# A kernel's activations in SBUF are allocated 64 bytes further from its weights

## The chip, the cores and the metric

The kernel runs on one core of a Trainium2 chip. The metric is the device time of one execution in microseconds (us). Three executions of the kernel before took 1510.82, 1510.87 and 1511.72 us, a median of 1510.87 us.

## What is computed

One layer of a hybrid decoder on 256 tokens of width 2048, in float32, and a final RMSNorm. Cut to its steps, the reference is:

```python
mod = silu(c) @ w_ada + b_ada           # shift1, scale1, gate1, shift2, scale2, gate2
h   = rms_norm(x, g_norm1) * (1 + scale1) + shift1
p   = h @ w_in                          # retention q,k,v,g | HGRN2 q,f,i,g | gates A, B
y_a = (layer_norm(retention(rope(q), rope(k), v)) * silu(g)) @ w_ret_o
y_b = (head_rms_norm(hgrn2(silu(q), f, i)) * silu(g)) @ w_hg_o
x   = x + gate1 * ((sigmoid(ga) * y_a + sigmoid(gb) * y_b) @ w_out)
h2  = rms_norm(x, g_norm2) * (1 + scale2) + shift2
a, b = split(causal_conv3(h2 @ w_up))   # w_up is 2048 x 11264
x   = x + gate2 * ((silu(a) * b) @ w_down)
out = rms_norm(x, g_final)
```

The weights are about 95 million float32 values, each read once (382 MB).

## The kernel before

**How a product is formed.** Weights and activations are both float32. Each is split into an upper part, which is the value rounded to the type float32r, and a lower part, which is what the rounding left out. A product is then three matmuls in float32r: upper activations by upper weights, lower activations by upper weights, and upper activations by lower weights. The upper and lower part of an activation lie side by side in one tile, for two blocks of 128 rows of the contraction: `hT` (after the first norm), `og` and `mT` (in the branches and their merge), `h2T` (after the second norm) and `gs` (in front of the down projection), each 128 partitions by 4096 bytes. The upper and lower parts of a weight piece are the tiles `wh` and `wl`, each also 128 by 4096 bytes, for two blocks of 128 rows and 512 columns.

**The flow of a weight piece.** `load` (L155) starts a DMA from HBM into a tile `raw` on the queue of SyncE. `upper` (L161) lets ScalarE copy it to `wh` with rounding (L169). `rest` (L172) lets VectorE subtract that from `raw` into `wl` (L174). `pieces` (L178) strings these together, `products` (L250) passes the pieces to one of the matmul helpers. A `raw` tile is free for its next load when L174 has read it; a `wh` or `wl` tile is free when the last matmul has read it.

**The matmul helpers.** In each, a matmul has a stationary operand, which a weight load brings into the array first, and a moving operand, which streams through it.

- `mm_rows` (L192): activations are stationary (128 columns), weights move (512 columns). L198 takes the upper activations, L199 the lower, both with `wh`; L203 takes the upper activations with `wl`. Most of the input projections and all of the output, merge and down projections use it.
- `mm_cols` (L205): weights stationary, activations moving, 256 columns (L214, L215, L218).
- `mm_wide` (L220): weights stationary, upper and lower activations together moving, 512 columns (L225), then the upper ones alone with `wl`, 256 columns (L228).
- `up_group` (L1110), the up projection: for each block of 128 rows and two column slices of the weights, two matmuls with `wh` and 512 moving columns (L1125) and two with `wl` and 256 (L1127).

So every one of these matmuls has one operand in a weight tile and one in an activation tile, and the weight load of the next matmul runs beside the stream of the current one.

**Other work.** The six modulation vectors are formed on VectorE by dot products (L458) that read a row of the modulation weights in `raw` and the vector `sc`. Retention and HGRN2 run in between on all engines, with float32 matmuls of their own that read activations alone: L711 multiplies a 128 by 128 block of scores (`at`) with the values (`p`), L713 another such block (`a`, from a pool of smaller tiles) with the same kind of values.

**Where the tiles lie.** SBUF is handed out pool after pool, and in a pool slot after slot, in the order in which a slot's tag is first used, each start rounded up to 32 bytes. All offsets are bytes within each partition. The constants come first, up to byte 17,440. Then comes the pool of weights, `self.wp` (L62): 12 slots of `raw`, each 4,128 bytes because the longest row has 1,025 float32 values, up to byte 66,976; then 4 slots of `wh` and 4 of `wl`, 4,096 bytes each, up to byte 99,744. There the pool of activations starts, `self.sb` (L63): 27 slots of 4,096 bytes (`blk`, L75) that hold all the activation tiles named above, then the smaller tiles (`small`, `s1`, `s2`).

The first `wh` slot and the first activation slot are therefore 32,768 bytes apart, 8 times 4,096. The slices that matmuls take start at multiples of 512 bytes within their tiles. So the starts of the two operands of any weight matmul are a multiple of 512 bytes apart.

The instructions are ordered by the program text, with the interleaved work metered by `pump` (L129); no step looks at an address.

Of the kernel before, what the change touches and what calls it, by code (L numbers as in the profile page):

```python
# [12 lines left out]
F32 = mybir.dt.float32  # L13
# [6 lines left out]
P = 128  # L20
# [37 lines left out]
class Kernel:  # L58
# [735 lines left out]
    def run(self):  # L794
# [29 lines left out]
        def take(g, ps, fresh):  # L824
            for at, z in self.parts(ps, ATT[g] in ROWS):
                dst = accs[g][:, at, :]
                if fresh:
                    nc.scalar.activation(dst, z, AF.Copy)
                else:
                    nc.vector.tensor_tensor(dst, dst, z, ALU.add)  # L830
# [44 lines left out]
        def begin(kind, hb, *ins):  # L875
            att.append(self.start(kind(hb, *ins, gates)))

        small = False
        while min(done) < KT:
            if work > SMALL and not small:  # L880
                small = True
                self.small_loads(nc.sync, ("freq", "lbT", "lmask"))
                self.start(self.trig())
                self.start(self.lower_bound())
            have = min(KT, 2 + int((work - LAG) / ADA_EVERY))
            m = have - done[g]
            if m > 0:
                self.finish(*ada[:have])
                if g < RESIDENT:
                    self.products(mms[g], ps[g], a["wa"][g], act, done[g], m, first=False, last=have == KT)  # L890
                    if have == KT:
                        take(g, ps[g], True)
                else:
                    take(g, self.products(mms[g], self.pg(), a["wa"][g], act, done[g], m), done[g] == 0)
                done[g] = have
                work += m
                if have == KT and ATT[g] in GATES:
                    nc.scalar.activation(accs[g], accs[g], AF.Silu)
                    gates[GATES.index(ATT[g])] = accs[g]
                for hb in range(2):  # L900
                    gs = [hb, 2 + hb, 4 + hb]
                    if g in gs and min(done[i] for i in gs) == KT:
                        self.pace(0, 14.0, 24)
                        begin(self.hgrn, hb, *(accs[i] for i in gs))
                        for i in gs:
                            accs[i] = None
            else:
                work += 0.5
            g = (g + 1) % len(ATT)
            if have == KT and done[0] < KT:  # L910
                g = min(i for i in range(len(ATT)) if done[i] < KT)
        self.xT = None
        v = accs[10:]
        del accs
# [377 lines left out]
```

## Time and profile before

| | |
|---|---|
| median of three executions | 1510.87 us |
| the profiled execution | 1511.24 us |
| its span, first to last instruction | 1509.5 us |
| PE (TensorE matmul) busy | 1493.7 us, 8,466 matmuls |
| PEld (weight load) busy | 1275.5 us |
| DVE (VectorE) busy | 1211.9 us |
| ACT (ScalarE) busy | 841.7 us |
| read from HBM | 382.11 MB, 255 GB/s over the span |
| mean granted TensorE clock | 0.998 |

The profiled execution is the one whose trace the sections below quote. Its span is 1.7 us shorter than its own time. A busy time counts the stretches in which at least one instruction of the engine is under way. A matmul's duration runs from its start to the modelled end of its output, so successive matmuls overlap in the trace: a mean of 395 ns does not mean that one starts each 395 ns. The rate is read from the chain of waits, which gives each matmul the time from its predecessor's end to its own.

### The profile page before, as it was taken

What the parts mean: (1) busy time and instruction counts of PE and PEld (TensorE: products, weight loads), DVE (VectorE), ACT (ScalarE), POOL (GpSimd) and SP (SyncE); (2) the same over time, 40 slices, a digit from 0 to 9 for tenths busy, and PEclk for the clock granted to TensorE, in tenths of its full rate; (3) what the DMA queues carried; (4) which work ended last, traced back from release to release, by engine and by line L of the source; (5) the groups of instructions that cost most, each with busy time, mean ns of one, the idle gap of its engine ahead of it and who ended that gap; (6) DMA issues with size and microseconds to landing.
All of it is one profiled execution on the core that took longest, in us unless ns stands there. A gap on an engine that the chain in (4) does not pass through costs nothing.

```text
span 1509.5 us, 22703 instructions
## 1 busy us (share of the span) xinstructions
PE 1493.7 (99%) x8466; PEld 1275.5 (84%) x8466; DVE 1211.9 (80%) x1647; ACT 841.7 (56%) x1210; POOL 4.0 (0%) x8
## 2 busy tenths in 40 slices
PE   8999999999999999999999999999999999999997
PEld 6889899888888888888888888888888888888886
DVE  7899997998999877898977778777777769455784
ACT  6745456767775644455466555555555658344342
POOL 0000000000000000000000000000000000000000
PEclk9999999999999999999999999999999999999999
DMA  9999997777887899989847777777777666667651
GB/s 373 376 347 336 321 320 257 265 248 274 281 278 262 285 302 326 318 290 361 298 132 242 229 233 230 230 231 238 229 239 231 216 193 204 197 206 212 183 171 56
DMA packets 110994, 385.71 MB, mean 256 GB/s; under 512 B 12802, under 2 KB 13346, under 8 KB 110884
## 3 DMA queue, kind: packets, MB, share of 16 engines
q1 hardware_dynamic: 110016, 383.14, 76.7%
q8 instruction: 66, 1.08, 0.3%
q10 hardware_dynamic: 868, 1.13, 0.2%
q14 instruction: 44, 0.36, 0.1%
HBM read 382.11 MB, written 2.11 MB: 255 GB/s over the span
## 4 chain that ended last, share of the span: by engine, by line
PE 93%; DVE 3%; ACT 1%; issue 1%; DMA 1%; SPq 0%; DVEq 0%; ACTq 0%
PE pg L198 13%; PE pg L203 13%; PE pg L199 13%; PE po L1125 11%; PE pg L1125 10%; PE po L1127 5%; PE pg L1127 5%; PE pg L225 4%; PE po L198 3%; PE po L203 3%; PE po L199 3%; PE pg L228 2%; DVE wl L174 1%; DVE raw L458 1%; PE po L218 1%
## 5 line engine op out<-in xcount | busy, mean ns | idle before, releaser
L174 DVE TENSOR_TENSOR wl<-raw,wh 128x1024 fp32r<-128x1024 f32 (+1 forms) x536 | 633.1, 1191 | 233.6 <-ACT wh L169 230.6
L169 ACT ACTIVATE wh<-raw 128x1024 fp32r<-128x1024 f32 (+1 forms) x536 | 547.9, 1033 | 482.5 <-PE pg L199 167.0
L458 DVE SCALAR_TENSOR_TENSOR raw<-raw,sc 128x1024 f32<-128x1024 f32 x192 | 233.8, 1222 | 0.1
L1125 PE MATMUL po<-h2T,wh 128*128 128x512 f32 x704 | 221.1, 395 | 0.0
L1125 PE MATMUL pg<-h2T,wh 128*128 128x512 f32 x688 | 216.4, 396 | 0.0
L198 PE MATMUL pg<-wh,hT 128*128 128x512 f32 x512 | 202.1, 395 | 0.9 <-DVE p L830 0.6
L199 PE MATMUL pg<-wh,hT 128*128 128x512 f32 x512 | 199.8, 390 | 0.0
L1127 PEld LDWEIGHTS po<-h2T,wl 128*128 128x128 f32 x704 | 132.3, 188 | 31.3
L1127 PEld LDWEIGHTS pg<-h2T,wl 128*128 128x128 f32 x688 | 129.2, 188 | 31.0 <-DVE wl L174 0.5
L203 PE MATMUL pg<-wl,hT 128*128 128x512 f32 x512 | 138.4, 390 | 0.1
L1127 PE MATMUL po<-h2T,wl 128*128 128x256 f32 x704 | 138.3, 278 | 0.0
L1127 PE MATMUL pg<-h2T,wl 128*128 128x256 f32 x688 | 135.3, 278 | 0.1
L198 PEld LDWEIGHTS pg<-wh,hT 128*128 128x128 f32 x512 | 96.1, 188 | 21.3 <-ACT f L579 1.0
L203 PEld LDWEIGHTS pg<-wl,hT 128*128 128x128 f32 x512 | 96.0, 188 | 20.6 <-DVE wl L174 0.4
L199 PEld LDWEIGHTS pg<-wh,hT 128*128 128x128 f32 x512 | 96.2, 188 | 19.6 <-DVE hT L387 0.3
L1125 PEld LDWEIGHTS po<-h2T,wh 128*128 128x128 f32 x704 | 107.2, 189 | 0.0
L1125 PEld LDWEIGHTS pg<-h2T,wh 128*128 128x128 f32 x688 | 104.7, 189 | 0.0
L199 PE MATMUL pg<-wh,gs 128*128 128x512 f32 x176 | 68.6, 390 | 0.0
L198 PE MATMUL pg<-wh,gs 128*128 128x512 f32 x176 | 68.5, 389 | 0.0
L198 PE MATMUL po<-wh,gs 128*128 128x512 f32 x176 | 68.5, 389 | 0.0
L199 PE MATMUL po<-wh,gs 128*128 128x512 f32 x176 | 68.5, 389 | 0.0
L225 PE MATMUL pg<-hT,wh 128*128 128x512 f32 x256 | 65.1, 396 | 0.2 <-DVE p L247 0.2
(255 smaller groups left out, 2023.3 us busy)
## 6 DMA issues: line engine op xcount, KB each, us to landing
raw<-in_wup SPq DMA_DIRECT2D x176, 512.0 KB, 4.5
raw<-in_wdown SPq DMA_DIRECT2D x88, 512.0 KB, 4.2
raw<-in_wa SPq DMA_DIRECT2D x80, 512.0 KB, 5.7
raw<-in_ada SPq DMA_DIRECT2D x64, 512.5 KB, 5.4
raw<-in_ada SPq DMA_DIRECT2D x64, 512.0 KB, 5.5
raw<-in_wab SPq DMA_DIRECT2D x64, 512.0 KB, 5.0
raw<-in_gate SPq DMA_DIRECT2D x32, 512.5 KB, 4.3
raw<-in_wk SPq DMA_DIRECT2D x32, 512.0 KB, 5.1
```

The source lines that it names most:

```text
L169: self.pin(self.nc.scalar.activation(wh, raw, AF.Copy))
L174: self.last = self.nc.vector.tensor_tensor(wl, raw, wh.bitcast(F32), ALU.subtract)
L198: nc.tensor.matmul(ps[t], lhsT=act[:, hi], rhs=wh, start=first and i == 0, stop=False)
L199: nc.tensor.matmul(ps[t], lhsT=act[:, lo], rhs=wh, start=False, stop=False)
L203: nc.tensor.matmul(ps[t], lhsT=act[:, hi], rhs=wl, start=False, stop=last and i == len(items) - 1)
L218: nc.tensor.matmul(outs[j], lhsT=wl[:, cs[j]], rhs=act[:, :T], start=False, stop=last and i == len(items) - 1, skip_group_check=True)
L225: nc.tensor.matmul(ps[z], lhsT=wh[:, z * P : (z + 1) * P], rhs=act, start=first and i == 0, stop=False)
L228: nc.tensor.matmul(ps[z][:, :T], lhsT=wl[:, z * P : (z + 1) * P], rhs=act[:, :T], start=False, stop=last and i == len(items) - 1)
L458: dot = self.pin(nc.vector.scalar_tensor_tensor(raw[:, 0, :], raw[:, 0, :], 1.0, self.sc[:, u * GW : u * GW + w], ALU.mult, ALU.mult, accu ...
L1125: self.pin(nc.tensor.matmul(ps[j + z], lhsT=wh[:, cs[z]], rhs=act, start=kt == 0, stop=False, skip_group_check=bool(begun)))
L1127: nc.tensor.matmul(ps[j + z][:, :T], lhsT=wl[:, cs[z]], rhs=act[:, :T], start=False, stop=kt == KT - 1, skip_group_check=bool(begun))
```

## The change

After the loop of the input projections, `run` takes one more tile from the pool of weights, 128 partitions by 16 float32 values, 64 bytes. Nothing writes or reads it.

```diff
@@ -909,6 +909,7 @@
             g = (g + 1) % len(ATT)
             if have == KT and done[0] < KT:
                 g = min(i for i in range(len(ATT)) if done[i] < KT)
+        self.wp.tile([P, 16], F32, name="gap")
         self.xT = None
         v = accs[10:]
         del accs
```

Its tag is new to the pool, so it gets a slot of its own behind the last `wl` slot, at byte 99,744, and every tile of the pool of activations starts 64 bytes later: the first activation slot is at byte 99,808, which is 8 times 4,096 and 64 bytes behind the first `wh` slot. Constants, `raw`, `wh`, `wl` and PSUM stay where they were. The last tile of the pool still ends within the same memory.

On each engine the list of instructions is the same as before, row by row: 5,592 rows on TensorE, 1,421 on VectorE, 1,158 on ScalarE, 764 on the queue of SyncE and 12 on GpSimd, with the same operations, shapes, waits and tile slots. What differs is the running number in tiles' names behind that point, the line numbers below L911, which are one higher, and the start addresses of the activation tiles.

## The prediction

> **What bounds the kernel now.** I read the page's totals and shares of the chain first, then the table by stage, the groups by shape, and the chain itself for the rate of the matmuls.
>
> ```profile
> span 1509.5 us, 22703 instructions
> PE 1493.7 (99%) x8466; PEld 1275.5 (84%) x8466; DVE 1211.9 (80%) x1647; ACT 841.7 (56%) x1210; POOL 4.0 (0%) x8
> ...
> PE 93%; DVE 3%; ACT 1%; issue 1%; DMA 1%; SPq 0%; DVEq 0%; ACTq 0%
> ```
>
> TensorE is under way in 1493.7 of 1509.5 us, and 93% of the chain that ended last are its matmuls. Only 15.8 us are not covered by it.
>
> ```profile
> 20.00:300.00 280.00, 278.33 (x1584) 245.04 (x1583) 251.24 (x329) 165.66 (x232) 1.91 (x2) 1.00 0.91 322
> ...
> 768.00:1185.00 417.00, 416.90 (x2418) 364.50 (x2417) 321.97 (x499) 240.63 (x367) 0.00 (x0) 1.00 0.72 226
> 1185.00:1509.50 324.50, 316.78 (x1501) 265.30 (x1499) 213.66 (x248) 154.12 (x199) 0.00 (x0) 0.99 0.59 180
> ```
>
> These are rows of the table by stage: stretch, its length, then busy time of PE, PEld, DVE, ACT and POOL, the granted clock, the DMA share and GB/s. In the input projections (20 to 300 us), in the up projection (from 768 us) and in the down projection, TensorE has the whole stretch but for 1.7, 0.1 and 7.7 us, the last being mostly the tail after the final matmul. The clock is full. No other engine is near its limit but VectorE in the first of these (251 of 280). So the time can change by more than about 1% only if the matmuls themselves start at another rate. How fast do they start?
>
> ```profile
> 299.98 0.84 PE pg L228 x7
> 300.81 1.84 PE pg L225 x8
> ...
> 1494.53 1.81 PE po L203 x8
> ```
>
> ```profile
> 900.01 0.46 PE po L1125 x2
> 900.48 0.23 PE po L1127 x2
> 900.71 0.47 PE po L1125 x2
> 901.18 0.23 PE po L1127 x2
> ...
> 905.59 0.46 PE pg L1125 x2
> ```
>
> These are rows of the chain: start, time taken, and what. 8 matmuls of 512 columns take 1.81 us, 0.2263 each; 7 of 256 columns take 0.84, 0.120 each. Twice the latter less the former is 0.0137 us: what each matmul costs beside its columns, 13.7 ns. In the up projection two of each kind should take 2 x 0.2263 + 2 x 0.120 = 0.6926 us. From 900.01 to 905.59 there are 16 rows, 8 such fours: 0.6975 each, about 0.005 more. This surplus and the 13.7 ns are the two places where a matmul may be waiting for its own operands.
>
> **The change part by part.** The extra tile has no instruction, no load and no semaphore, and each engine's list is the same row by row. So nothing is removed, added or moved past a queue, and the sum has no term for an instruction. What is left is the address of the activations: absolute (64 bytes more) and relative to the weights and the constants. It can act only where an instruction's duration depends on addresses. I go through the kinds.
>
> *VectorE and ScalarE on weights.* Their operands lie in one pool and move in no way.
>
> ```profile
> L174 DVE TENSOR_TENSOR wl<-raw,wh x536: 670/1224/1271, 17.4 to 1491.1; 128x1024 fp32r<-128x1024 f32 x167, 128x512 fp32r<-128x512 f32 x12
> ...
> L169 ACT ACTIVATE wh<-raw x536: 616/1062/1074, 15.3 to 1490.0; 128x1024 fp32r<-128x1024 f32 x167, 128x512 fp32r<-128x512 f32 x12
> ...
> L458 DVE SCALAR_TENSOR_TENSOR raw<-raw,sc x192: 1194/1221/1261, 10.9 to 1186.3; 128x1024 f32<-128x1024 f32 x96, 128x1025 f32<-128x1025 f32 x96
> ```
>
> Here stand shortest, median and longest duration in ns. They also test the question itself. The 12 `raw` slots are 4,128 bytes apart, so from slot to slot the distance to `wh`, `wl` and `sc` shifts by 32 bytes beyond a multiple of 4,096; over the slots all distances modulo 128 occur in equal number, the 64 bytes of this change among them. If one in four were slower or faster the medians would not lie this near one end: 1,224 of at most 1,271 for L174 (its low end is the half-sized form), 1,221 between 1,194 and 1,261 for L458. So VectorE and ScalarE do not feel such a distance by more than about 3%, and where they work on activations I cost the shift at zero. The cover is TensorE's 99%: VectorE has 29 us free between 20 and 300 us, and 3% of its 251 us is 7.5.
>
> *DMA.* Nearly all bytes go to `raw`, which stays; the few loads and stores of activations keep their sizes. Zero, between -1 and +1 us for the last stores in the tail.
>
> *TensorE on weights.* All of the weights' matmuls, some 7,470 of the 8,466, pair a weight tile with an activation tile. Today their starts are a multiple of 512 bytes apart, then a multiple of 512 and 64. No row of this trace shows that distance with float32r operands, so I bound it. The nearest row by address is in the branch:
>
> ```profile
> 358.50 0.39 PE L711 MATMUL po<-p,at 128*128 128x128 f32 x2
> 358.73 0.39 PE L713 MATMUL po<-p,a 128*128 128x128 f32 x2
> 358.95 0.39 PE L711 MATMUL po<-p,at 128*128 128x128 f32 x2
> 359.17 0.39 PE L713 MATMUL po<-p,a 128*128 128x128 f32 x2
> ```
>
> In L711 both operands are in 4,096-byte slots, a multiple of 512 bytes apart. In L713 the stationary one is in a smaller pool whose slots lie 32 bytes off that grid modulo 64 and 96 modulo 128. Both lines take 0.39 us for two and start 0.22 to 0.23 us apart. So the distance does not matter there. The nearest row by kind is the down projection: within a tile L198, L199 and L203 use stationary slices at 0, 512, 1024 and 1536 bytes, and the 1.81 us for 8 has no room for a slow one among them. I take zero, the value of both nearest rows. The weakness is that the first is float32 and slower per column, and the second moves by 512 only, so an effect that repeats within 512 bytes would be hidden.
>
> By the Trainium skill, "TensorE: Matmul & The Clock Gate", section "Step-by-step: what each phase is for", TensorE has two independent read ports into SBUF, one for the moving operand and one for the weight load, so a weight load takes nothing from the running matmul; by that rule the distance is free and the sum is zero. The same page's "Back-to-back issue gap" gives 2.5 ns beside the columns at the full clock; this trace shows 13.7, so here the trace does not agree.
>
> *Sum.* 0 on 1511.24 us, the profiled execution's own time (its span and 1.74 us around it). That execution lies 0.37 us above the median of the three, within their spread of 0.9, so the forecast for the median is **1510.9 us**.
>
> **The rivals.**
>
> *Somewhat faster: the surplus goes.* The 0.005 us in each four of the up projection, and its like elsewhere, could be weight loads that meet the stream at the same low addresses, as all now do.
>
> ```profile
> L1125 PE MATMUL po<-h2T,wh 128*128 128x512 f32 x704 | 221.1, 395 | 0.0
> L1125 PE MATMUL pg<-h2T,wh 128*128 128x512 f32 x688 | 216.4, 396 | 0.0
> L198 PE MATMUL pg<-wh,hT 128*128 128x512 f32 x512 | 202.1, 395 | 0.9 <-DVE p L830 0.6 <-ACT p L828 0.2
> L198 PE MATMUL po<-wh,gs 128*128 128x512 f32 x176 | 68.5, 389 | 0.0
> L225 PE MATMUL pg<-hT,wh 128*128 128x512 f32 x256 | 65.1, 396 | 0.2 <-DVE p L247 0.2
> ```
>
> These are groups by shape: total and mean ns of one. There are (704 + 688) / 2 = 696 fours: 696 x 0.005 = 3.5 us. L225 takes 1.84 us for 8 against 1.81: 32 x 0.03 = 1 us. L198 on `hT` has a mean of 395 against 389 on `gs`: 512 x 0.006 = 3 us. Together 7.5. That gives 1507.4 for the up projection alone and 1503.4 for all. For it: such a surplus appears in lines where the activations move. Against it: L198 on `hT` has it too and is of the other kind, and in the up projection 512 and 256 columns alternate, so it may be the alternation.
>
> *Much faster: the 13.7 ns go.* If each weight load now delays the stream because both read the same place, the shift could end that: at most 7,470 x 0.0137 = 102 us, 1409 us. For it: the distance is the same for every weight matmul, as is the cost. Against it: L711 and L713. By the page's figure of 2.5 ns instead of none, it would be about 84 us, an estimate.
>
> *Slower: the weight load meets the stream where it didn't.* The place is every steady run of L198 to L203 and L214 to L228, which now has the clean rate. It decides from the point where one more matmul in each four is delayed as in the up projection: 0.005 / 4 = 0.00125 us on the 7,470 - 2,784 = 4,690 other matmuls, 5.9 us, 1516.8. If instead each took the 0.23 of L225's rows (1.84 / 8), 0.0037 x 5,000 matmuls of 512 columns, 18.5 us, 1529.4. For it: with all starts on one grid a weight load keeps a fixed place relative to the stream, and the clean rate may rest on that place. Against it: the same rows as above.
>
> *The change does not do what it says.* The tile could be placed where it shifts nothing. The start addresses in the built program speak against it; the time would be 1510.9.
>
> **How the numbers follow.** The addresses do not matter: 0.51, with 0.03 for the shift that isn't one, together 0.54 at 1510.9. Somewhat faster 0.20, at 1503.4 to 1507.4. Much faster 0.06. Slower 0.20, of which I put two thirds at 1516.8 and a little beyond. A measurement of this kernel can tell about 0.2%, 3 us, from no change; both ends of the first rival and of the third are past that, so faster is 0.26, same 0.54, slower 0.20. The range goes from the first rival's far end, less a little, to the third's near end and 2 us for its spread: 1503 to 1519. Outside lie the much faster case and the far third of the slower one, 0.06 + 0.07 = 0.13.
>
> **What would show it.** In the changed kernel's chain, 8 matmuls of L203 should take 1.81 us again and the fours of the up projection 0.6975. The first rival is right if the fours fall towards 0.693 and L198's mean on `hT` towards 389; the second if L203's 8 fall below 1.81, towards 1.72; the third if they rise, or if L199's mean passes 389. L174, L169 and L458 should keep 1,224, 1,062 and 1,221. The forecast is wrong if, with an identical list of instructions, TensorE's busy time in the up or down projection changes by more than 1 us. It would also be wrong, for another reason, if the 7.7 us that the last stretch leaves uncovered grew, since no operation there changed.

## The result and the profile after

The changed kernel took 1524.64 us (median of four executions, 1524.3 to 1525.71) against 1511.21 us for the kernel before on the same chips: a ratio of 1.009, 95% interval 1.0077 to 1.0102. It is slower, by 13.4 us. The forecast was no change, 1510.9 us, with a range of 1503 to 1519 that does not hold the time.

The page of the changed kernel, its totals and shares of the chain:

```profile
span 1522.8 us, 22703 instructions
PE 1507.6 (99%) x8466; PEld 1273.4 (84%) x8466; DVE 1212.3 (80%) x1647; ACT 841.6 (55%) x1210; POOL 4.0 (0%) x8
...
PE 96%; ACT 2%; DVE 1%; issue 0%; DMA 0%; SPq 0%; DVEq 0%; ACTq 0%
```

VectorE and ScalarE are busy as long as before, to 0.4 us, and the granted clock is 0.998 in both kernels. TensorE is busy 13.9 us longer with the same 8,466 matmuls, and the span is 13.3 us longer. So no wait was added: matmuls themselves start later after one another. Rows of the chain (start, time taken, what) show which:

```profile
300.54 1.83 PE pg L225 x8
302.37 0.91 PE pg L228 x8
...
1507.66 1.87 PE po L203 x8
```

```profile
900.16 0.46 PE po L1126 x2
900.62 0.23 PE po L1128 x2
...
905.68 0.46 PE po L1126 x2
```

Eight matmuls of L203 take 1.87 us instead of 1.81, those of L225 1.83 instead of 1.84. The up projection (lines L1126 and L1128 here) has 16 rows from 900.16 to 905.68, eight fours in 5.52 us: 0.690 each instead of 0.6975. One kind of line became slower, the other faster. The groups by shape, total us and mean ns of one, agree:

```profile
L1126 PE MATMUL po<-h2T,wh 128*128 128x512 f32 x704 | 218.4, 392 | 0.0
L198 PE MATMUL pg<-wh,hT 128*128 128x512 f32 x512 | 204.5, 399 | 0.9 <-ACT wh L169 0.6 <-ACT p L828 0.3
L198 PE MATMUL po<-wh,gs 128*128 128x512 f32 x176 | 70.0, 398 | 0.0
L199 PE MATMUL po<-wh,gs 128*128 128x512 f32 x176 | 69.2, 393 | 0.0
L225 PE MATMUL pg<-hT,wh 128*128 128x512 f32 x256 | 65.1, 397 | 0.3 <-DVE p L247 0.3
```

L198 on `gs` went from 389 to 398 ns, L1126 from 395 to 392. The operations that split the weights, on operands that did not move against each other, kept their medians (shortest, median and longest ns):

```profile
L174 DVE TENSOR_TENSOR wl<-raw,wh x536: 665/1224/1260, 17.1 to 1504.1; 128x1024 fp32r<-128x1024 f32 x167, 128x512 fp32r<-128x512 f32 x12
L169 ACT ACTIVATE wh<-raw x536: 613/1062/1074, 14.7 to 1503.0; 128x1024 fp32r<-128x1024 f32 x167, 128x512 fp32r<-128x512 f32 x12
```

For a balance I took, for each matmul of both traces, the time from its start to the start of the next, subtracted before from after, and added up by helper; such a time includes whatever the next matmul waited for. The up projection is that of `up_group`. The same balance is used for the experiments below (all in us, against the trace of before):

| kernel | mm_rows (3,360) | mm_cols (768) | mm_wide (512) | up projection (2,784) | others | sum |
|---|---|---|---|---|---|---|
| changed kernel | +20.4 | -1.7 | -0.5 | -4.5 | -0.4 | +13.3 |
| e1_all_shift | 0.0 | -0.1 | 0.0 | 0.0 | -0.1 | -0.2 |
| e2_room | +0.1 | 0.0 | 0.0 | 0.0 | -0.2 | -0.1 |
| e3_nearer64 | +6.3 | -4.1 | -0.4 | -2.3 | 0.0 | -0.5 |
| e4_sweep32 | +16.8 | -1.5 | +0.4 | +2.4 | 0.0 | +18.0 |
| e5_rows_back | +0.2 | -1.3 | -0.6 | -4.6 | 0.0 | -6.5 |
| e6_up_only | +0.1 | -0.1 | 0.0 | -4.6 | -0.2 | -4.7 |
| e7_best | +0.2 | -1.9 | -0.6 | -4.6 | -0.2 | -7.2 |
| e8_sweep_fine | +17.5 | -1.2 | +0.1 | +2.0 | -0.1 | +18.2 |
| e9_gap128 | +18.8 | -0.8 | +0.4 | 0.0 | -0.4 | +18.1 |
| e10_dist256 | 0.0 | +1.1 | 0.0 | 0.0 | +0.1 | +1.1 |
| e11_up_wl | +0.1 | -0.1 | 0.0 | -2.3 | 0.0 | -2.3 |
| e12_up_wh | +0.1 | 0.0 | 0.0 | +1.1 | -0.3 | +0.8 |

In the changed kernel the lines with stationary activations lost 20.4 us, 6.1 ns a matmul, and those with stationary weights won 6.7 back.

### The profile page after: what moved, and what is told of

Read it like the earlier page. It is cut to its first block, busy times and chain, and to the rows that moved or that the text cites. A ratio compares the mean times of both kernels' runs of the same rounds, so it can differ in the third digit from the quotient of the medians.

```text
span 1522.8 us, 22703 instructions
## 1 busy us (share of the span) xinstructions
PE 1507.6 (99%) x8466; PEld 1273.4 (84%) x8466; DVE 1212.3 (80%) x1647; ACT 841.6 (55%) x1210; POOL 4.0 (0%) x8
## 4 chain that ended last, share of the span: by engine, by line
PE 96%; ACT 2%; DVE 1%; issue 0%; DMA 0%; SPq 0%; DVEq 0%; ACTq 0%
PE pg L198 14%; PE pg L199 14%; PE pg L203 14%; PE po L1126 11%; PE pg L1126 10%; PE po L1128 5%; PE pg L1128 5%; PE pg L225 4%; PE po L198 3%; PE po L203 3%; PE po L199 3%; PE pg L228 2%; PE po L214 1%; PE po L215 1%; PE po L218 1%; PE pg L214 1%
## 5 line engine op out<-in xcount | busy, mean ns | idle before, releaser
L174 DVE TENSOR_TENSOR wl<-raw,wh 128x1024 fp32r<-128x1024 f32 (+1 forms) x536 | 632.7, 1189 | 242.1 <-ACT wh L169 239.8
L169 ACT ACTIVATE wh<-raw 128x1024 fp32r<-128x1024 f32 (+1 forms) x536 | 547.8, 1033 | 498.2 <-PE pg L199 186.9
L1126 PE MATMUL po<-h2T,wh 128*128 128x512 f32 x704 | 218.4, 392 | 0.0
L1126 PE MATMUL pg<-h2T,wh 128*128 128x512 f32 x688 | 213.9, 392 | 0.0
L198 PE MATMUL pg<-wh,hT 128*128 128x512 f32 x512 | 204.5, 399 | 0.9 <-ACT wh L169 0.6
L199 PE MATMUL pg<-wh,hT 128*128 128x512 f32 x512 | 202.7, 396 | 0.0
L1128 PEld LDWEIGHTS po<-h2T,wl 128*128 128x128 f32 x704 | 132.2, 188 | 29.1
L1128 PEld LDWEIGHTS pg<-h2T,wl 128*128 128x128 f32 x688 | 129.1, 188 | 29.0 <-DVE wl L174 0.6
L203 PE MATMUL pg<-wl,hT 128*128 128x512 f32 x512 | 141.5, 395 | 0.0
L1128 PE MATMUL po<-h2T,wl 128*128 128x256 f32 x704 | 138.9, 279 | 0.0
L1128 PE MATMUL pg<-h2T,wl 128*128 128x256 f32 x688 | 136.0, 279 | 0.1
L198 PEld LDWEIGHTS pg<-wh,hT 128*128 128x128 f32 x512 | 96.1, 188 | 24.0 <-ACT wh L169 1.0
L203 PEld LDWEIGHTS pg<-wl,hT 128*128 128x128 f32 x512 | 96.0, 188 | 23.4
L199 PEld LDWEIGHTS pg<-wh,hT 128*128 128x128 f32 x512 | 96.1, 188 | 22.7 <-DVE hT L387 0.2
L1126 PEld LDWEIGHTS po<-h2T,wh 128*128 128x128 f32 x704 | 106.6, 188 | 0.0
L1126 PEld LDWEIGHTS pg<-h2T,wh 128*128 128x128 f32 x688 | 104.2, 188 | 0.0
L198 PE MATMUL po<-wh,gs 128*128 128x512 f32 x176 | 70.0, 398 | 0.0
L198 PE MATMUL pg<-wh,gs 128*128 128x512 f32 x176 | 70.0, 398 | 0.0
L199 PE MATMUL pg<-wh,gs 128*128 128x512 f32 x176 | 69.3, 393 | 0.0
L199 PE MATMUL po<-wh,gs 128*128 128x512 f32 x176 | 69.2, 393 | 0.0
L225 PE MATMUL pg<-hT,wh 128*128 128x512 f32 x256 | 65.1, 397 | 0.3 <-DVE p L247 0.3
```

The source lines that it names most:

```text
L169: self.pin(self.nc.scalar.activation(wh, raw, AF.Copy))
L174: self.last = self.nc.vector.tensor_tensor(wl, raw, wh.bitcast(F32), ALU.subtract)
L198: nc.tensor.matmul(ps[t], lhsT=act[:, hi], rhs=wh, start=first and i == 0, stop=False)
L199: nc.tensor.matmul(ps[t], lhsT=act[:, lo], rhs=wh, start=False, stop=False)
L203: nc.tensor.matmul(ps[t], lhsT=act[:, hi], rhs=wl, start=False, stop=last and i == len(items) - 1)
L225: nc.tensor.matmul(ps[z], lhsT=wh[:, z * P : (z + 1) * P], rhs=act, start=first and i == 0, stop=False)
```

## The experiments

A time that is given without a ratio is that of a single execution; the kernel before took 1511.1 us (median) beside each of these groups of runs.

**Distance or place?** Two theories fit this. By the distance theory, the rate of a weight matmul depends on how far its two operands lie apart. By the place theory, it depends on where the activations lie, whatever the weights do. e1_all_shift moves both pools by the same 64 bytes:

```diff
+        c.tile([P, 16], F32, name="gap")
         self.silu = []
```

> The 64 bytes are put among the constants, so weights and activations both start 64 bytes later and their distance is that of before. Distance theory (a weight matmul's rate depends on the distance between its stationary and its moving operand): as before, 1511 us, L198 on gs 389 ns mean, L1125 395 to 396. Place theory (the rate depends on where the activations lie, whatever the weights do): as the changed kernel, 1524.6 us, L198 on gs 398, L1125 392.

It took 1510.96 us beside 1511.13 for the kernel before. Its groups are those of before:

```profile
L1126 PE MATMUL po<-h2T,wh 128*128 128x512 f32 x704 | 221.1, 395 | 0.0
...
L198 PE MATMUL po<-wh,gs 128*128 128x512 f32 x176 | 68.5, 389 | 0.0
```

The activations lie exactly where the changed kernel has them, and nothing is slower. The place theory falls.

**A base in which the distance can be set.** To set distances by helper, the slots of `wh` and `wl` get room, and each piece starts at an offset in its slot:

```diff
-        raw = self.wp.tile([P, m, w], F32, name=f"raw_{self.n}", tag="raw", bufs=12)
+        raw = self.wp.tile([P, m, w], F32, name=f"raw_{self.n}", tag="raw", bufs=11)
...
+    def offset(self, kind):
+        return "", {}.get(kind, 0)
+    def place(self, name, tag, o, m, w):
+        z = self.wp.tile([P, 2 * G + 128], F32R, name=f"{name}_{self.n}", tag=tag, bufs=4)
+        return z[:, o : o + m * w].rearrange("p (m w) -> p m w", m=m)
...
+        z, o = self.offset(kind)
+        wh = self.place("wh" + z, "wh", o, m, w)
+        wl = self.place("wl" + z, "wl", o, m, w)
```

`kind` says which helper will use the piece: rows, cols, wide or up. Offsets count float32 values, so 16 is 64 bytes. A weight that starts further into its slot lies nearer to the activations behind it: an offset of 192 or 448 bytes leaves the activations 64 bytes beyond a multiple of 256, as in the changed kernel. In these kernels L198, L199 and L203 have become L207, L208 and L212, and L1125 and L1127 have become L1135 and L1137.

> Gives each wh and wl slot 512 bytes more (4608 instead of 4096) and takes one of the twelve raw slots for it; the distances stay multiples of 512, and 32 bytes among the constants keep the weights' own place modulo 512. Both theories: 1511 us within 2 us, L198 on gs 389, L1125 395 to 396. It is the base for the next two; if the eleventh raw slot costs, it shows here.

1511.18 us, with all five columns of the balance within 0.2 us of before. The missing `raw` slot costs nothing.

**The other direction.** e3_nearer64 puts all weights at 64 bytes: `{"rows": 16, "cols": 16, "wide": 16, "up": 16}`.

> As e2_room, but weights start 64 bytes further into their slots in all stages, so that the activations lie 64 bytes nearer to them instead of further. Distance theory with a sign (the changed kernel slowed the lines with stationary activations by 4 to 9 ns a matmul and sped up those with stationary weights by 2 to 4): the roles are exchanged; L1125 should be slower than before and the lines L198 to L203 faster or at least not slower, about 1500 to 1512 us. Distance theory without a sign: as the changed kernel, 1524 us, L198 on gs 398. Place theory: as before, 1511 us, since no activation moved.

1510.64 us. The simple exchange of roles did not happen, and neither did the changed kernel's loss:

```profile
L1135 PE MATMUL po<-h2T,wh 128*128 128x512 f32 x704 | 219.6, 393 | 0.0
...
L208 PE MATMUL po<-wh,gs 128*128 128x512 f32 x176 | 69.0, 392 | 0.0
...
L207 PE MATMUL po<-wh,gs 128*128 128x512 f32 x176 | 68.9, 391 | 0.0
```

`mm_rows` is slower than before, but by 6.3 us and not by 20.4; the up projection and `mm_cols` are faster. A time equal to that of before hides a loss and gains of the same size. The direction of the distance matters, but not as a mirror.

**A sweep in one execution.** e4_sweep32 lets the offset go through 16 values of 32 bytes each from piece to piece and puts a letter into the tiles' names, so that the profile keeps them apart.

```diff
+        i = self.turns = getattr(self, "turns", -1) + 1
+        i = (5 * i + i // 16) % 16
+        return "ABCDEFGHIJKLMNOP"[i], 8 * i
```

> As e2_room, but each weight piece starts at another of 16 offsets in its slot, 0 to 480 bytes in steps of 32 (letters A to P in the names wh and wl). Distance theory: the groups of one line by letter differ, for L198 on gs between at least 389 (A) and 398 (448 bytes, letter O, the distance of the changed kernel), and the letters that are best for stationary activations are not those that are best for stationary weights (L1125). Place theory: all letters of a line have the same mean, within 1 ns.

1529.0 us. Rows for the matmuls with `wl` and `hT` (L214 here; shortest, median, longest ns) and groups of the up projection (L1137 here; total us, mean ns), by letter:

```profile
L214 PE MATMUL pg<-wlI,hT x30: 389/389/397, 34.6 to 584.1; 128*128 128x512 f32 x30
L214 PE MATMUL pg<-wlC,hT x36: 388/392/398, 40.2 to 589.7; 128*128 128x512 f32 x36
L214 PE MATMUL pg<-wlK,hT x36: 388/392/397, 65.3 to 567.4; 128*128 128x512 f32 x36
L214 PE MATMUL pg<-wlB,hT x38: 393/395/397, 46.2 to 553.5; 128*128 128x512 f32 x38
L214 PE MATMUL pg<-wlJ,hT x36: 393/396/400, 117.1 to 575.8; 128*128 128x512 f32 x36
```

```profile
L1137 PE MATMUL po<-h2T,whA 128*128 128x512 f32 x48 | 15.0, 394 | 0.0
L1137 PE MATMUL po<-h2T,whC 128*128 128x512 f32 x48 | 15.2, 397 | 0.0
L1137 PE MATMUL po<-h2T,whG 128*128 128x512 f32 x40 | 12.4, 392 | 0.0
L1137 PE MATMUL po<-h2T,whK 128*128 128x512 f32 x40 | 12.6, 397 | 0.0
L1137 PE MATMUL po<-h2T,whO 128*128 128x512 f32 x48 | 14.9, 392 | 0.0
```

The letters differ. Letters eight places apart, 256 bytes, agree: C with K, B with J, G with O. In L214, with stationary activations, 0 and 256 bytes (A, I) are the best, and the odd multiples of 32 are among the slow ones. With stationary weights 192 and 448 (G, O) are better than 0. G also repeats the loss of the changed kernel, though no activation moved: L198 and L199 on `gs` (L209 and L210 here) have medians of 398 and 393 ns, the means of the changed kernel.

```profile
L209 PE MATMUL pg<-whG,gs x12: 392/398/398, 1279.8 to 1440.0; 128*128 128x512 f32 x12
L210 PE MATMUL pg<-whG,gs x12: 388/393/393, 1280.0 to 1440.2; 128*128 128x512 f32 x12
```

By the spacing of starts within a piece, a four of the up projection takes 696 ns at A, 690 at G and 706 at F; `mm_cols` seemed best at C and at G, 113 ns a matmul against 120 at A. The means of one letter are contaminated by neighbouring pieces that lie elsewhere, so only kernels with one distance a helper, as below, give clean figures.

**The loss undone, the gain kept.** If distance it is, one can have the old distance for `mm_rows` and the new one for the rest.

```diff
+        return "", {"cols": 48, "wide": 48, "up": 48}.get(kind, 0)   # e5_rows_back
+        return "", {"up": 48}.get(kind, 0)                           # e6_up_only
+        return "", {"cols": 16, "wide": 48, "up": 48}.get(kind, 0)   # e7_best
```

> As e2_room, with the weights of mm_cols, mm_wide and the up projection starting 192 bytes into their slots (for these the distance of the changed kernel, if the pattern repeats every 256 bytes as the letters of e4_sweep32 do: A like I, G like O) and those of mm_rows at 0, the distance of before. Distance theory: the changed kernel without its loss. L198 on gs back at 389, L1125 near 392 as there; 1511.2 less the 6 to 7 us that the lines with stationary weights gained, 1504 to 1506 us. Place theory: 1511, as no activation moved.

1504.67 us, a ratio to before of 0.9955 (0.9939 to 0.9971). It beats both kernels, by 6.4 us and by 20 us, with the same 8,466 matmuls.

```profile
L1135 PE MATMUL po<-h2T,wh 128*128 128x512 f32 x704 | 218.4, 392 | 0.0
...
L207 PE MATMUL po<-wh,gs 128*128 128x512 f32 x176 | 68.5, 389 | 0.0
```

> As e2_room, with only the up projection's weights at 192 bytes. Distance theory: the up projection's share alone, 4 to 5 us off, 1506 to 1507 us; all other lines as in e2_room. If the gain of one stage is given back by another that starts earlier (loads that come late), less than 2 us.

1506.7 us, 0.9971 (0.9958 to 0.9985): 4.4 us off, as large as the up projection's own column, 4.6. Nothing is given back.

> As e5_rows_back, but the weights of mm_cols at 64 bytes, where letter C of e4_sweep32 gave starts 113 ns apart instead of 120. Distance theory: 768 matmuls x 4 to 7 ns more, 3 to 5 us below e5_rows_back, 1500 to 1502 us. If the input projections, where VectorE is busy 90% of the time and the DMA engines 91%, can't use a faster TensorE, no difference to e5_rows_back.

1504.73 us, 0.9958 (0.9944 to 0.9972), no better than e5_rows_back. The reason is not the one offered: `mm_cols` itself hardly became faster. In the rows of its first line (L223; shortest, median, longest ns), e5_rows_back, e7_best and then e3_nearer64, which has the same 64 bytes there:

```profile
L223 PE MATMUL pg<-hT,wh x128: 279/279/415, 21.2 to 264.4; 128*128 128x256 f32 x128
```

```profile
L223 PE MATMUL pg<-hT,wh x128: 276/281/281, 20.7 to 263.6; 128*128 128x256 f32 x128
```

```profile
L223 PE MATMUL pg<-hT,wh x128: 276/276/342, 21.1 to 263.0; 128*128 128x256 f32 x128
```

At one and the same distance, the median is 281 in e7_best and 276 in e3_nearer64. The two also differ in where the pieces of `mm_rows` lie, whose matmuls alternate with those of `mm_cols` in stretches of about 100 to 200. That does not explain it: by the spacing of starts, the first stretch of `mm_cols`, before any matmul of `mm_rows`, already has a median of 118 ns in e7_best and of 114 in e3_nearer64. Of the four long stretches after it, e7_best has three at 118 and one at 114, e3_nearer64 all four at 113. And the sweep's 113 ns for G, the distance of `mm_cols` in e5_rows_back, became 118 there. So at one distance, in one execution, a run of matmuls can keep either of two rates, and the distance alone does not fix the rate. What picks one is not shown.

**Finer steps.** e8_sweep_fine is e4_sweep32 with other offsets.

```diff
-        return "ABCDEFGHIJKLMNOP"[i], 8 * i
+        return "ABCDEFGHIJKLMNOP"[i], (0, 1, 2, 3, 4, 12, 15, 16, 17, 20, 28, 36, 44, 48, 52, 60)[i]
```

> As e4_sweep32, with offsets that are no multiples of 32 (letters A to P: 0, 4, 8, 12, 16, 48, 60, 64, 68, 80, 112, 144, 176, 192, 208, 240 bytes). If the distance counts in whole units of 16 bytes, B, C and D equal A, and I equals H; if in units of 64, the letters fall into four groups by the nearest multiple below; if every byte counts, all differ.

1529.3 us. For the same line as above, 4 bytes (B), 8 (C), 68 (I), 64 (H) and 12 (D):

```profile
L214 PE MATMUL pg<-wlB,hT x38: 394/402/403, 46.1 to 554.0; 128*128 128x512 f32 x38
L214 PE MATMUL pg<-wlC,hT x36: 389/395/400, 40.0 to 590.2; 128*128 128x512 f32 x36
L214 PE MATMUL pg<-wlI,hT x30: 398/402/405, 34.4 to 584.6; 128*128 128x512 f32 x30
L214 PE MATMUL pg<-wlH,hT x30: 388/392/397, 41.9 to 592.9; 128*128 128x512 f32 x30
L214 PE MATMUL pg<-wlD,hT x26: 389/390/393, 183.1 to 581.8; 128*128 128x512 f32 x26
```

In this sweep four bytes are enough: 402 ns against the 389 that multiples of 256 have. More is not worse: 12 bytes have 390. There is no unit of 16 or 64 bytes within which the distance does not matter.

**Period.**

> The changed kernel with a tile of 128 bytes instead of 64. Distance theory with the letters of e4_sweep32 (E: 128 bytes): the 3,360 matmuls of L198 to L203 start about 232 ns apart instead of 226.7, 18 us; the up projection's fours take 699.7 instead of 696.2 ns, 2.4 us more; mm_cols gains 1: about 1530 us, slower than the changed kernel, L198 on gs 394 or more. If what counts is that 64 is no multiple of 128 (the place of a tile in a unit of 128 bytes), as before: 1511 us.

e9_gap128 is the changed kernel with `[P, 32]` for the extra tile. 1528.91 us, 1.0114 (1.0085 to 1.0144), where about 1530 was expected: `mm_rows` lost 18.8 us (18 expected), the up projection nothing (2.4 expected).

```profile
L199 PE MATMUL po<-wh,gs 128*128 128x512 f32 x176 | 70.0, 398 | 0.0
L198 PE MATMUL po<-wh,gs 128*128 128x512 f32 x176 | 69.0, 392 | 0.0
```

> As e2_room with all weights 256 bytes into their slots, so that all distances are 256 bytes off. If the pattern repeats every 256 bytes: 1511 us, L198 on gs 389, L1125 395 to 396. If it repeats only at 512 or more, another time, by several us.

e10_dist256 sets all four offsets to 64 values, 256 bytes. 1512.32 us; `mm_rows`, `mm_wide` and the up projection are those of before to the tenth of a microsecond, `mm_cols` is 1.1 us slower, all of it in its first 96 matmuls; after these its starts are 120 ns apart as before. So the rate is the same again after 256 bytes, and by e9_gap128 it is not after 128.

**Which two accesses meet?** The weight load of the next matmul runs beside the current stream; or a matmul's own stationary and moving operand could matter. In the up projection the upper and lower weights can be moved apart from each other. e11_up_wl and e12_up_wh are e6_up_only with, respectively, `wh` and `wl` kept at 0:

```diff
-        wh = self.place("wh" + z, "wh", o, m, w)
+        wh = self.place("wh" + z, "wh", 0, m, w)   # e11_up_wl
-        wl = self.place("wl" + z, "wl", o, m, w)
+        wl = self.place("wl" + z, "wl", 0, m, w)   # e12_up_wh
```

> As e6_up_only, but only the lower weights wl of the up projection lie at 192 bytes, the upper ones wh at 0. In the program's order the weight loads under way during the four matmuls are wh, wl, wl, wh. If the load of the next weights meets the current stream, half of the loads move: L1125 about 393.7 ns, half the gain, 1508.5 to 1509 us. If a matmul meets its own weights' place, L1125 stays at 395 to 396 and only L1127 changes: 1510.5 to 1512 us.

> The counterpart of e11_up_wl: only the upper weights wh lie at 192 bytes. If the load of the next weights meets the current stream: again half, L1125 about 393.7 ns, 1508.5 to 1509 us. If a matmul meets its own weights' place: L1125 at 392, nearly the whole gain, 1506 to 1507 us.

e11_up_wl took 1508.8 us, 0.9986 (0.9974 to 0.9997), half of the gain. e12_up_wh took 1515.88 us, 1.0031 (1.0018 to 1.0044). Groups of e11_up_wl, then of e12_up_wh:

```profile
L1135 PE MATMUL po<-h2T,wh 128*128 128x512 f32 x704 | 219.1, 392 | 0.0
L1137 PE MATMUL po<-h2T,wl 128*128 128x256 f32 x704 | 139.3, 279 | 0.0
```

```profile
L1135 PE MATMUL po<-h2T,wh 128*128 128x512 f32 x704 | 220.3, 394 | 0.0
L1137 PE MATMUL po<-h2T,wl 128*128 128x256 f32 x704 | 139.9, 280 | 0.0
```

A matmul's own weights are not what counts alone: with `wh` where it was, L1135 went from 395 to 392, and with `wh` moved alone it did not get there. The next load meeting the stream fits e11_up_wl well. There, the mean time (without the few that hold a longer wait) from the second matmul with `wh` to the first with `wl`, during which a load of `wl` runs, fell from 233.4 in e2_room to 228.6 ns, and the time between the two with `wh` stayed near (232.9 and 231.8). It fits e12_up_wh less: the time between the two with `wh`, during which the moved `wh` is loaded, fell to 230.4, against 227.5 with both moved, but the fours became longer as a whole, 698.5 ns against 696.9. The halves do not add up to the whole, -2.3 and +1.1 us against -4.6. The eight executions of e12_up_wh also spread from 1512.0 to 1518.3 us, where e11_up_wl has 1508.6 to 1510.1; that is not explained, and the trace, with +0.8 us, is of an execution at the low end of that spread (1512.16 us). So a collision of the weight load with the stream is likely and not shown, and its rule in detail stays open.

## Why the prediction was wrong

*What bounds the kernel* was right. TensorE has all of the span before and after, and the time moved only because its matmuls started at another rate; the span grew by 13.3 us and TensorE's busy time by 13.9.

*No term for an instruction, VectorE, ScalarE and DMA at zero* was right. VectorE and ScalarE are busy as long as before, to 0.4 us, and e1_all_shift, which moves both pools against PSUM and against the first constants, shows nothing. The argument by medians was weaker than it looked. L174 and L169 pair operands that do not move against each other here, so their medians had to stay; and one slot in four could be slower without moving a median. What bounds the effect are the longest durations, 1,271 and 1,261 ns against medians of 1,224 and 1,221, 3 to 4%.

*TensorE on weights at zero* was the step that failed: "I take zero, the value of both nearest rows." The term is +20.4 us for stationary activations and -6.7 us for stationary weights. The prediction had named the weakness, that an effect which repeats within 512 bytes would be hidden, and did not let it weigh: the pattern repeats every 256 bytes, so slices 512 bytes apart were all at one and the same point of it, and the clean 1.81 us for 8 was no sample of distances but one distance, which happens to be the best of those tried for `mm_rows`. The other row, L711 against L713, compared distances that do differ, but in float32 matmuls of 128 columns at a lower rate per column; it says nothing for float32r streams. Why float32 does not show it was not tried. Nearest by address and nearest by kind were each far in the other respect, and two such rows do not make one near row.

*The rule that weight loads take nothing from the stream.* The Trainium skill, "TensorE: Matmul & The Clock Gate", section "Step-by-step: what each phase is for", says that a weight load does not take read bandwidth from the running matmul. What the prediction drew from it, that the distance is free, does not hold: a matmul of L198 on `gs` takes 389 or 398 ns with nothing changed but the distance, and the measurement decides. Whether the weight load is what takes the time is not shown.

*Somewhat faster* was right in size for its own place, the up projection. The surplus there was a matter of distance, not of the alternation of 512 and 256 columns: the fours of the chain fell from 0.6975 to 0.690 us, below the 0.6926 that was taken for the clean rate, and the balance has 4.5 us in all against the 3.5 forecast. That the cause is weight loads that meet the stream, as this rival said, is not shown. Elsewhere it failed: L198 on `hT`, which it had falling towards 389 ns, went from 395 to 399.

*Slower* was the rival that came true, at the place it named for `mm_rows` and not for `mm_cols` and `mm_wide`, which got faster. Its condition held: the clean rate of `mm_rows` rested on the distance. Its price ran from 5.9 to 18.5 us. The 20.4 us of `mm_rows` alone lie beyond the far end, because each of its 3,360 matmuls lost 6.1 ns where the far end put 3.7; and of the 5,000 matmuls that the far end counted, 1,392 of the up projection and 256 of L225 had the slower rate already. The range took in only the near end and 2 us, up to 1519, and so missed 1524.6.

*Much faster* did not happen: in no kernel here is the column of `mm_rows` below that of before by as much as 0.1 us. (The weight matmuls are 7,440, not 7,470, which changes no term.) But the 13.7 ns are no fixed cost of a matmul either. They were worked out from the 120 ns of L228, and in e3_nearer64 the same line (L237 there) starts after a median of 113 ns; twice 113 less 226.7 leaves nothing.

## What to carry to other kernels

When TensorE bounds a kernel like this one, in float32r and with a weight load for every matmul, the distance between the weight tiles and the activation tiles, modulo 256 bytes here, is a tuning parameter: it alone moved this kernel between 1504.7 us (e5_rows_back) and 1528.9 (e9_gap128). Any tile or padding added between two pools sets it unseen, while one ahead of both (e1_all_shift) does not. Set it for each kind of matmul, as e5_rows_back does, because the best distance for stationary activations is not the one for stationary weights. And before a clean rate is taken as proof that something doesn't matter, ask whether the trace holds more than one value of it.

## What was not expected of the hardware

- Two float32r operands 4 bytes off a multiple of 256 already slow the stream: medians of 402 (e8_sweep_fine) against 389 ns for a matmul of 512 columns. At 12 bytes off it is 390. Both are from a sweep; no kernel had 4 bytes throughout.
- The rates come in steps, and one distance can hold two of them. With stationary activations the starts in the down projection are 226.7 ns apart at distance 0; in the changed kernel they are 231 apart after L199 and 236 after L198, in turn.
- A matmul of 256 columns with stationary weights can follow its predecessor after 113 ns as well as after 120 (`mm_cols`, medians of 276 and 283 ns in e3_nearer64 and e2_room), and the distance does not decide alone which: e7_best has stretches of 118 and of 114 ns at the distance at which e3_nearer64 has 113 to 114.
